# Sixteen transfers inside SBUF in place of a write to DRAM and four reads, for the shifted rows of a depthwise convolution

## The chip, the cores and the metric

One core of a Trainium2 chip runs the kernel. The metric is device time in microseconds, the median of several runs. The profile is of one execution; its times are microseconds from the start of its span. Engines: PE is TensorE, DVE is VectorE, ACT is ScalarE, POOL is GpSimd, SP is the engine from which most transfers are issued (SPq is its queue in the profile).

## The reference

Two layers over 512 tokens of 1024 channels. The change lies in the convolution module of the first layer; what follows it (SwiGLU feed-forward, attention, a second feed-forward) is untouched.

```
def conformer_conv(x, w_pw1, b_pw1, w_dw, b_dw, ln_g, ln_b, w_pw2, b_pw2):
    a = jax.nn.glu(x @ w_pw1 + b_pw1, axis=-1)
    y = lax.conv_general_dilated(                 # depthwise, causal, 31 taps
        a, w_dw[:, None, :].astype(a.dtype), window_strides=(1,),
        padding=((CONV_WIDTH - 1, 0),),
        dimension_numbers=('NWC', 'WIO', 'NWC'),
        feature_group_count=D_MODEL) + b_dw
    y = jax.nn.silu(layernorm(y, ln_g, ln_b))
    return y @ w_pw2 + b_pw2
...
h = h + conformer_conv(rmsnorm(h, norm_mix[l]), ...)
```

For a channel c and a token s the convolution is y[s, c] = sum over j of w[j, c] * apad[c, s + j], where apad is the gated row of the channel with 30 zeros ahead of it.

## The kernel before

Activations lie with channels on the 128 partitions and tokens along the free dimension, so 1024 channels are 8 tiles (numbered 0 to 7, `ct` in the code) of 128x512. Matrix products are made in float32 by three matmuls on a high and a low part of each operand. The weights come in chunks of 128x1024 floats (512 KB), loaded from DRAM into one of four buffers named `raw` (issued from SP, line 285), then split by ACT (`whi`, line 307, a cast) and by DVE (`wlo`, line 307, a subtraction). PE uses the chunks in a fixed order; the first pointwise product uses chunks 2*ct and 2*ct+1 for tile ct, sixteen in all, and the second the next eight. A buffer `raw` can be filled again when its chunk is split.

For each tile, `project` makes the pointwise product in two PSUM banks (PE, line 375, the line of the helper that keeps PE's order), and `gate` makes the gated rows `apad` of 128x542 floats from them (DVE lines 917, 919 and 920, ACT line 918). The 31 taps of a tile are then shared out:

- DVE makes the first taps one by one (`taps`, recorded on line 318, the line of a helper `Turn` that sets an order among operations of one kind).
- ACT and POOL make the next ones (`products`, ACT lines 970 and 973, POOL line 975).
- PE makes the last 12 to 20 in `rounds` (line 956), four taps by one matmul. For this it needs the tile's rows in a second layout, the tile `shifted`: partition s*32+c of column block g holds channel g*32+c, moved by s tokens. A matmul then multiplies 128 rows (32 channels, four shifts) with a 128x32 table. Tile 7 adds four taps by diagonal matrices (`diagonals`) and does its rounds by halves.

`shifted` is made by transfers alone: channels must move to other partitions. In the kernel before, `gate` issues from SP a write of `apad` to a DRAM tile `rowsd`, and then four reads of it, one for each shift s, each into 32 partitions. All of these go through the helper `copies`, a `Turn`, and so stand on line 318. There are four buffers of `shifted` and three of `apad`.

The order of PE's work in this stage is the order of the code: project(0), project(1), project(2) with rounds(0) at its end, then project(3), (4), (5) with rounds(1), (2), (3) each in the second half, then project(6), project(7), rounds(4), (5), (6), the diagonals, sums for the layer norm, and rounds(7). On the other engines and on SP a scheduler sets the order when the program is built. Each engine takes its instructions strictly in that order, and SP takes its transfers so too: one that waits holds up all behind it. The transfers from SP and ACT take their completion semaphores from eight in turn, and a transfer is issued only when the last one with its semaphore has landed, so at most eight are under way.

Of the kernel before, what the change touches and what calls it, by code (L numbers as in the profile page):

```python
# [10 lines left out]
F32 = mybir.dt.float32  # L11
# [6 lines left out]
P = 128  # L18
D = 1024
S = 512  # L20
# [4 lines left out]
PAD = TAPS - 1  # L25
# [159 lines left out]
def hybrid_trunk(ctx: ExitStack, tc: tile.TileContext, xT, W, prm_in, wdw_in, rnd_in, sinks, relb, onehot, fin, out):  # L185
    nc = tc.nc
# [6 lines left out]
    dpool = ctx.enter_context(tc.tile_pool(name="dram", bufs=1, space=DRAM))  # L193
# [3 lines left out]
    def uid(s):  # L197
        ctr[0] += 1
        return f"{s}{ctr[0]}"
# [7 lines left out]
    def temp():  # L207
        return tmp.tile([P, 512], F32, tag="tmp", name=uid("tmp"))
# [234 lines left out]
    def col(name, i):  # L443
        c = PARAM_COLS[name] + i
        return prm[:, c:c + 1]
# [351 lines left out]
    with conv_stage:  # L797
# [58 lines left out]
        for k in range(KT):  # L856
            g = col("mix0", k)
# [26 lines left out]
        copies = Turn()  # L884

        class Conv:
# [24 lines left out]
            def gate(self):  # L911
                ct = self.ct
                rs_bc = rms0.step2()
                a = self.a = cv.tile([P, PAD + S], F32, tag="apad", name=uid("apad"), bufs=3)
                nc.gpsimd.memset(a[:, 0:PAD], 0.0)
                sig = temp()
                nc.vector.tensor_mul(sig, self.gt, rs_bc)
                gated = nc.scalar.activation(sig, sig, AF.Sigmoid, bias=col("b1", KT + ct)).ins
                nc.vector.tensor_mul(self.lin, self.lin, rs_bc)
                self.gated = nc.vector.scalar_tensor_tensor(a[:, PAD:], self.lin, col("b1", ct), sig, op0=ALU.add,  # L920
                                                            op1=ALU.mult).ins
                n = S + 4 * (self.r - 1)
                q = self.q = cv.tile([P, 4, S + 4 * (max(ROUNDS) - 1)], F32, tag="shifted", name=uid("shifted"), bufs=4)
                row = PAD + S
                ad = dpool.tile([P, row], F32, tag=uid("rows"), name=uid("rowsd"))
                copies(nc.sync.dma_start, ad, a)
                for s in range(4):
                    copies(nc.sync.dma_start, q[s * 32:(s + 1) * 32, :, 0:n],
                           bass.AP(tensor=ad.tensor, offset=ad.offset + self.j0 + s,
                                   ap=[[row, 32], [32 * row, 4], [1, n]]))  # L930
                for n in range(self.n_diag):
                    with tc.issue_after(gated):
                        nc.scalar.mul(diag[:, n, :], ident, self.tap(TAPS - self.n_diag + n))
# [555 lines left out]
```

## Time and profile before

| What | Value |
|---|---|
| Median of 3 runs | 1037.89 us (1037.68 to 1038.6) |
| Profiled execution | 1037.62 us, of which 1035.8 us are the span of instructions |
| Granted TensorE clock | 0.999 |
| PE busy | 1023.2 us (99% of the span) |
| DVE, ACT, POOL busy | 815.9, 544.4, 222.1 us |
| Convolution stage on PE | about 11 to 148 us of the span |
| Transfers `rowsd<-apad` | 8, of 271 KB, median 2.6 us from issue to landing |
| Transfers `shifted<-rowsd` | 32, of 260 to 264 KB, medians 4.4 to 5.6 us |

Busy time is the share in which an engine worked; for a kernel whose PE is busy 99% of the time the question for any edit is which PE idle time it removes or adds. Rows of the timeline give start, duration, engine, line, operation, `out<-in`, and in brackets the idle time of the engine before it with what ended it. "To landing" is the time from a transfer's issue to its completion.

### The profile page before, as it was taken

To read this page: it belongs to the slowest core of one execution; us is meant where nothing else is said; L and a number is where in the kernel's file an instruction comes from. 1 tells how busy PE (TensorE), PEld (TensorE's weight loads), DVE (VectorE), ACT (ScalarE), POOL (GpSimd) and SP (SyncE) were. 2 spreads that over 40 slices of the span, in tenths; PEclk is the share of its full clock that TensorE was granted. 3 is DMA by queue.
4 is the path that set the end of the run, shared out by engine and by line. 5 is a ranking of instruction groups with operands and counts; after the bars stand their busy time and mean duration, and the time that the engine had idled before them with its cause. 6 is when DMAs were issued, how large, how long until landed. Compare 5 with 4: busy or idle time off the path is not lost.

```text
span 1035.8 us, 17669 instructions
## 1 busy us (share of the span) xinstructions
PE 1023.2 (99%) x7016; PEld 912.4 (88%) x7016; DVE 815.9 (79%) x1144; ACT 544.4 (53%) x847; POOL 222.1 (21%) x249
## 2 busy tenths in 40 slices
PE   8999999999999999999999999999999999999997
PEld 7766568888999999999998778788989999999996
DVE  7889867589789888988997677578956888789863
ACT  7566745434554555455565666344534654555443
POOL 0799811311001010010000534141200001010000
PEclk9999999999999999999999999999999999999999
DMA  7766542366557975785473120641664459666612
GB/s 242 204 158 159 131 129 82 108 177 163 153 137 190 269 185 142 234 209 138 102 235 92 61 62 21 178 110 38 162 223 129 117 137 261 187 147 171 178 41 82
DMA packets 51055, 153.95 MB, mean 149 GB/s; under 512 B 5979, under 2 KB 8844, under 8 KB 50956
## 3 DMA queue, kind: packets, MB, share of 16 engines
q1 hardware_dynamic: 41756, 124.79, 38.1%
q0 software_dynamic: 8064, 26.74, 15.0%
q10 hardware_dynamic: 1152, 1.29, 0.4%
q8 instruction: 55, 0.90, 0.3%
q14 instruction: 28, 0.23, 0.1%
HBM read 148.46 MB, written 6.83 MB: 150 GB/s over the span
## 4 chain that ended last, share of the span: by engine, by line
PE 93%; DMA 3%; DVE 2%; ACT 1%; issue 0%; SPq 0%; DVEq 0%; ACTq 0%
PE bank L383 23%; PE bank L384 23%; PE bank L385 23%; PE bank L375 21%; PE bank L1418 2%; DMA rowsd<-apad 1%; DVE wlo L307 1%; DMA h<-in_xT_dram 1%; DMA shifted<-rowsd 1%; ACT tmp L318 0%; DMA raw<-in_W_dram 0%; PE bank L1408 0%; ACT quad L318 0%; DMA prm<-in_prm_dram 0%; ACT whi L307 0%
## 5 line engine op out<-in xcount | busy, mean ns | idle before, releaser
L384 PE MATMUL bank<-quad,whi 128*128 128x256 f32 (+1 forms) x1572 | 472.4, 302 | 0.0
L385 PE MATMUL bank<-quad,wlo 128*128 128x256 f32 (+1 forms) x1572 | 469.6, 302 | 0.0
L383 PE MATMUL bank<-quad,whi 128*128 128x256 f32 (+1 forms) x1572 | 465.7, 302 | 0.0
L384 PEld LDWEIGHTS bank<-quad,whi 128*128 128x128 f32 x1572 | 300.0, 191 | 11.1
L383 PEld LDWEIGHTS bank<-quad,whi 128*128 128x128 f32 x1572 | 298.4, 191 | 11.2
L385 PEld LDWEIGHTS bank<-quad,wlo 128*128 128x128 f32 x1572 | 298.2, 191 | 11.0
L307 ACT CAST whi<-raw 128x1024 fp32r<-128x1024 f32 (+1 forms) x184 | 184.0, 1002 | 214.2 <-PE bank L384 123.3
L307 DVE TENSOR_TENSOR wlo<-raw,whi 128x1024 fp32r<-128x1024 f32 (+1 forms) x184 | 224.9, 1227 | 82.5 <-ACT whi L307 79.8
L375 PE MATMUL bank<-quad,whi 128*128 128x512 f32 x512 | 161.0, 395 | 2.4 <-ACT whi L318 0.9
L241 POOL DMA_DIRECT2D blocks<-in_W_dram x56 | 49.5, 907 | 460.6 <-DMA blocks<-in_W_dram 169.3
L307 ACT CAST whi<-blocks 128x1024 fp32r<-128x1024 f32 (+1 forms) x84 | 81.6, 972 | 111.3 <-PE bank L384 81.8
L375 PEld LDWEIGHTS bank<-quad,whi 128*128 128x128 f32 x512 | 94.4, 188 | 29.1 <-issue 5.1
L307 DVE TENSOR_TENSOR wlo<-blocks,whi 128x1024 fp32r<-128x1024 f32 (+1 forms) x84 | 94.1, 1124 | 10.1 <-ACT whi L307 9.3
L375 PE MATMUL bank<-quad,wlo 128*128 128x512 f32 x256 | 99.9, 390 | 0.1
L975 POOL TENSOR_TENSOR quad<-quad 128x512 f32<-128x512 f32 x53 | 76.6, 1445 | 13.3 <-ACT quad L973 10.2
L375 PEld LDWEIGHTS bank<-quad,wlo 128*128 128x128 f32 x256 | 48.0, 188 | 10.9 <-DVE wlo L318 0.7
L611 DVE TENSOR_TENSOR h<-h,bank 128x512 f32<-128x512 f32 x70 | 46.8, 680 | 10.7 <-PE bank L385 10.6
L973 ACT ACTIVATE quad<-apad,wdw 128x512 f32<-128x512 f32 x53 | 36.9, 718 | 20.0 <-POOL quad L975 20.0
L1317 POOL TENSOR_SCALAR sc<-sc,sm 128x256 f32<-128x256 f32 (+1 forms) x64 | 31.8, 519 | 58.9 <-DVE sm L1315 58.8
L517 DVE TENSOR_TENSOR quad<-tmp,quad 128x512 fp32r<-128x512 f32 (+1 forms) x62 | 41.0, 662 | 2.3 <-ACT quad L516 2.1
L516 ACT CAST quad<-tmp 128x512 fp32r<-128x512 f32 (+1 forms) x62 | 35.1, 584 | 13.7 <-POOL tmp L655 7.6
L1313 ACT ACTIVATE sc<-sc,m 128x257 f32<-128x257 f32 (+1 forms) x64 | 30.3, 475 | 22.2 <-DVE m L1304 22.2
(192 smaller groups left out, 1216.2 us busy)
## 6 DMA issues: line engine op xcount, KB each, us to landing
raw<-in_W_dram SPq DMA_DIRECT2D x109, 512.0 KB, 3.8
blocks<-in_W_dram SPq DMA_DIRECT2D x54, 512.0 KB, 6.0
blocks<-in_W_dram POOLq DMA_DIRECT2D x36, 512.0 KB, 7.6
blocks<-in_W_dram SPq DMA_DIRECT2D x30, 384.0 KB, 3.9
raw<-in_W_dram SPq DMA_DIRECT2D x21, 384.0 KB, 3.7
blocks<-in_W_dram POOLq DMA_DIRECT2D x20, 384.0 KB, 5.9
shifted<-rowsd SPq DMA_DIRECT2D x16, 262.0 KB, 4.4
shifted<-rowsd SPq DMA_DIRECT2D x12, 260.0 KB, 5.3
```

Source lines behind the costliest of these rows:

```text
L241: nc.gpsimd.dma_start(f[:, j, 0:w], part(1 - j, 1 - j), accum_op=ALU.add)
L307: done = (nc.scalar.copy(hi, r).ins, lo_engine[0].tensor_sub(lo, r, f32(hi)).ins)
L375: turn[0] = nc.tensor.matmul(*args, **kw).ins
L383: nc.tensor.matmul(out, w[0], x[0], start=start, stop=False, **kw)
L384: nc.tensor.matmul(out, w[0], x[1], start=False, stop=False, **kw)
L385: nc.tensor.matmul(out, w[1], x[0], start=False, stop=stop, **kw)
L516: nc.scalar.copy(dst[0], src)
L517: nc.vector.tensor_sub(dst[1], src, f32(dst[0]))
L611: nc.vector.tensor_tensor(t, t, src.rearrange("p (m s) -> p m s", m=2), op=op)
L973: nc.scalar.mul(pr, src, self.tap(j))
L975: nc.gpsimd.tensor_add(to, acc, pr)
L1317: nc.gpsimd.tensor_scalar(sc[:, j, 1:1 + w], sc[:, j, 1:1 + w], sm[:, j:j + 1], 0.0, op0=ALU.mult, op1=ALU.add)
```

## The change

The write to DRAM and the four reads are taken out. In their place stand sixteen transfers from `apad` to `shifted`, one for each shift s and each block g of 32 channels, 32 rows of 2080 to 2112 bytes each. The three lines on `rowsd` go.

```
                 q = self.q = cv.tile([P, 4, S + 4 * (max(ROUNDS) - 1)], F32, tag="shifted", name=uid("shifted"), bufs=4)
-                row = PAD + S
-                ad = dpool.tile([P, row], F32, tag=uid("rows"), name=uid("rowsd"))
-                copies(nc.sync.dma_start, ad, a)
                 for s in range(4):
-                    copies(nc.sync.dma_start, q[s * 32:(s + 1) * 32, :, 0:n],
-                           bass.AP(tensor=ad.tensor, offset=ad.offset + self.j0 + s,
-                                   ap=[[row, 32], [32 * row, 4], [1, n]]))
+                    for g in range(4):
+                        copies(nc.sync.dma_start, q[s * 32:(s + 1) * 32, g, 0:n],
+                               a[g * 32:(g + 1) * 32, self.j0 + s:self.j0 + s + n])
```

The scheduler puts some instructions in another order. PE's order is the same in both programs. On SP, from the copies of tile 0 to those of tile 2, these rows stand before (raw_439, 469, 559 and 589 are chunks 9 to 12, raw_682 and raw_712 chunks 13 and 14; apad_334, 400 and 513 are tiles 0, 1 and 2):

```order
L318 DMA rowsd_342<-apad_334 128x542
L285 DMA raw_439<-in_W_dram 128x1024
L318 DMA shifted_341<-rowsd_342 32x4x520 x4
L285 DMA raw_469<-in_W_dram 128x1024
L285 DMA raw_559<-in_W_dram 128x1024
L285 DMA raw_589<-in_W_dram 128x1024
L318 DMA rowsd_408<-apad_400 128x542
L318 DMA shifted_407<-rowsd_408 32x4x524 x4
L285 DMA raw_682<-in_W_dram 128x1024
L318 DMA rowsd_521<-apad_513 128x542
L285 DMA raw_712<-in_W_dram 128x1024
L318 DMA shifted_520<-rowsd_521 32x4x520 x4
```

After the change the same stretch of SP reads so (raw_459, 489, 589, 619 are chunks 9 to 12, raw_722 and raw_752 chunks 13 and 14; apad_334, 410 and 533 are tiles 0, 1 and 2):

```order
L318 DMA shifted_341<-apad_334 32x520 x16
L318 DMA shifted_417<-apad_410 32x524 x16
L285 DMA raw_459<-in_W_dram 128x1024
L285 DMA raw_489<-in_W_dram 128x1024
L285 DMA raw_589<-in_W_dram 128x1024
L285 DMA raw_619<-in_W_dram 128x1024
L285 DMA raw_722<-in_W_dram 128x1024
L285 DMA raw_752<-in_W_dram 128x1024
L318 DMA shifted_540<-apad_533 32x520 x16
```

Chunks 9 to 12, which went out ahead of tile 1's copies, now stand behind all 32 transfers of tiles 0 and 1, and chunk 14 moved ahead of tile 2's copies.

On DVE, around the gating of tile 2 (line 920 with apad_513), these rows stand before; wlo_592 and wlo_685 are the low parts of chunks 9 and 10, and line 992 adds the rounds of tile 0:

```order
L307 TENSOR_TENSOR wlo_592<-raw_439,whi_591 128x1024
L917 TENSOR_TENSOR tmp_515<-bank_438,rsbc_182 128x512
L919 TENSOR_TENSOR bank_437<-bank_437,rsbc_182 128x512
L920 SCALAR_TENSOR_TENSOR apad_513<-bank_437,prm,tmp_515 128x512
L307 TENSOR_TENSOR wlo_685<-raw_469,whi_684 128x1024
```

After the change (line 992 is line 989 there) they read:

```order
L917 TENSOR_TENSOR tmp_535<-bank_458,rsbc_182 128x512
L307 TENSOR_TENSOR wlo_622<-raw_459,whi_621 128x1024
L919 TENSOR_TENSOR bank_457<-bank_457,rsbc_182 128x512
L307 TENSOR_TENSOR wlo_725<-raw_489,whi_724 128x1024
L920 SCALAR_TENSOR_TENSOR apad_533<-bank_457,prm,tmp_535 128x512
```

The split of chunk 10 now stands ahead of tile 2's gating instead of behind it, and line 917 ahead of the split of chunk 9.

## The prediction

> **What bounds the kernel now.** I read the page first, then who PE waited for in the convolution stage, then the busy time by stretch.
>
> ```profile
> PE 1023.2 (99%) x7016; PEld 912.4 (88%) x7016; DVE 815.9 (79%) x1144; ACT 544.4 (53%) x847; POOL 222.1 (21%) x249
> ```
>
> PE is the bound: all its idle time in the span is 1035.8 - 1023.2 = 12.6 us. Only idle time that hangs on these copies can be won. In the stretch from 20 to 150 us PE's waits are:
>
> ```profile
> PE bank L375 <- DMA shifted<-rowsd: 1.2, 2, 0.9
> PE bank L534 <- ACT quad L318: 0.8, 1, 0.8
> PE bank L375 <- DVE mv L318: 0.3, 1, 0.3
> ```
>
> The columns are total, count and longest. The copies cost PE 1.2 us in two waits. Busy time by stretch (window, its length, PE busy, and so on) shows nothing else hidden:
>
> ```profile
> 43.00:62.00 19.00, 18.05 (x105) 10.90 (x106) 14.94 (x20) 11.22 (x16) 17.20 (x15) 1.00 0.63 177
> 62.00:130.00 68.00, 68.00 (x366) 42.85 (x365) 60.84 (x74) 44.63 (x66) 63.30 (x48) 1.00 0.62 153
> 20.00:150.00 130.00, 127.83 (x736) 84.94 (x735) 108.10 (x134) 76.46 (x111) 94.48 (x71) 1.00 0.62 161
> ```
>
> From 62 to 130 us PE has no gap at all. The whole stage has 130 - 127.83 = 2.17 us of idle time. PE's starts of the rounds are the deadlines of the copies:
>
> ```profile
> 43.71 2.78 PE L375 MATMUL bank<-shifted,tables 128*32 128x512 f32 x24 [0.91 <-DMA shifted<-rowsd]
> 55.16 3.64 PE L375 MATMUL bank<-shifted,tables 128*32 128x512 f32 x32 [0.24 <-DMA shifted<-rowsd]
> 70.83 2.78 PE L375 MATMUL bank<-shifted,tables 128*32 128x512 f32 x24
> 86.43 3.64 PE L375 MATMUL bank<-shifted,tables 128*32 128x512 f32 x32
> 118.76 9.65 PE L375 MATMUL bank<-shifted,tables 128*32 128x512 f32 x88
> 134.62 0.66 PE L375 MATMUL bank<-shifted,tables 128*32 128x256 f32 x8
> ```
>
> The rows are tiles 0, 1, 2, 3, then 4 to 6 together, then 7. Only tiles 0 and 1 came late, by 0.91 and 0.24 us, 1.15 us together. That is the most that copies which are early enough can give; the rest of the span follows PE, so it is carried to the end.
>
> **What the old copies cost.** SP's queue (x is the number of issues in the row; its duration is theirs):
>
> ```profile
> 31.85 0.33 SPq L318 DMA_DIRECT2D rowsd<-apad  x1
> 34.16 1.76 SPq L318 DMA_DIRECT2D shifted<-rowsd  x4
> 36.04 3.00 SPq L285 DMA_DIRECT2D raw<-in_W_dram  x3
> 40.06 0.33 SPq L318 DMA_DIRECT2D rowsd<-apad  x1
> 47.80 1.76 SPq L318 DMA_DIRECT2D shifted<-rowsd  x4
> 59.23 0.34 SPq L318 DMA_DIRECT2D rowsd<-apad  x1
> 61.81 1.74 SPq L318 DMA_DIRECT2D shifted<-rowsd  x4
> 73.63 0.35 SPq L285 DMA_DIRECT2D raw<-in_W_dram  x1
> 74.33 0.34 SPq L318 DMA_DIRECT2D rowsd<-apad  x1
> 114.49 0.34 SPq L318 DMA_DIRECT2D rowsd<-apad  x1
> 124.31 0.34 SPq L318 DMA_DIRECT2D rowsd<-apad  x1
> 126.67 1.73 SPq L318 DMA_DIRECT2D shifted<-rowsd  x4
> 131.41 27.08 SPq L285 DMA_DIRECT2D raw<-in_W_dram  x6
> ```
>
> A write goes out as soon as the rows are gated. Undisturbed, the reads follow 2.3 to 2.6 us later; tile 1's write at 40.06 stood behind the three weight loads of the row at 36.04, and its reads waited until 47.80. The rate of tile 1's reads, from the DMA view of 47.8 to 55.2 us in 40 slices of 0.185 us:
>
> ```profile
> GB/s 0 0 0 0 0 125 34 159 181 385 374 363 227 238 181 227 181 181 181 193 193 272 238 227 227 238 181 227 181 193 159 125 68 45 0 0 0 0 0 0
> DMA packets 576, 1.07 MB, mean 145 GB/s; under 512 B 64, under 2 KB 64, under 8 KB 576
> ```
>
> Data begins about 0.9 us after the first issue, moves mostly at some 200 GB/s, ends near 54.0, and PE starts at 55.16: 7.2 us from first issue to use. So the old way needs 2.4 + 7.2 = 9.6 us after gating, undisturbed.
>
> **The new copies.** Each is a quarter of a read, 66.6 KB: 0.33 us of data at 200 GB/s. No transfer inside SBUF is in this trace, so issue and landing are bounded by the nearest rows:
>
> ```profile
> L318 SPq DMA_DIRECT2D shifted<-rowsd x32: 302/424/433, 34.2 to 128.0; - x32
> DMA to landing us min/median/max: 3.4/5.2/7.2
> rowsd<-apad SPq DMA_DIRECT2D x8, 271.0 KB, 2.6
> raw<-in_W_dram SPq DMA_DIRECT2D x16, 512.0 KB, 4.5
> raw<-in_W_dram SPq DMA_DIRECT2D x2, 512.0 KB, 6.0
> ```
>
> The first row is issue time in ns, the second the landing of the same reads; the two last are weight loads, all of 20 to 135 us and those of 39 to 58 us, in a fuller queue. Issue spacing: 0.35 us (0.302 plus a gap of 0.05) to 0.46 us (1.76 us for four, and a little for the semaphore); I take 0.40, nearer the simple rows of 0.33 to 0.34. Landing: from 2.3 us (the lowest of the writes, as the gap 31.85 to 34.16 shows) to 3.4 us (the lowest of the 262 KB reads). I take 2.4, which is 3.4 less the 0.98 us that the other three quarters take at 200 GB/s. With eight semaphores in turn the ninth issue waits for the first landing: 8 x 0.40 = 3.2 us is above 2.4, so no wait. Sixteen copies then land 15 x 0.40 + 2.4 = 8.4 us after gating, bounds 7.6 and 10.3.
>
> The Trainium skill speaks against this: "DMA: Bandwidth & Descriptors", Rules for kernel authors, says to coalesce small transfers, since near 64 KB one pays mostly overhead, and its section on the anatomy of one DMA puts 2.0 us fixed on each, an estimate of 2.15 us for 66.6 KB. By that landing the sixteen would take 8.15 us instead of 8.4; that the fixed part overlaps is borne out here by four reads in 7.2 us.
>
> Tile by tile, with PE 1.15 us earlier from tile 1 on:
> - Tile 0: 31.85 + 8.4 = 40.3 (upper 42.2), needed at 43.71 - 0.91 = 42.8. Its stall goes, also at the upper bound.
> - Tile 1: SP is free at 38.3, so 40.06 + 8.4 = 48.5, needed at 54.0. Its stall goes.
> - Chunks 9 to 12, which stand behind these 32 copies: issued from 40.06 + 16 x 0.40 = 46.5, so chunk 9 lands at 46.5 + 4.5 = 51.0. ACT casts it when its products are done, as before (below, at 53.87). Hidden, by 2.9 us.
> - Tile 2 is the tightest. Rows of ACT and DVE there:
>
> ```profile
> 53.87 1.03 ACT L307 CAST whi<-raw 128x1024 fp32r<-128x1024 f32 x1
> 54.93 2.08 DVE L307 TENSOR_TENSOR wlo<-raw,whi 128x1024 fp32r<-128x1024 f32 x1 [3.33 <-ACT whi L307]
> 56.94 0.68 DVE L917 TENSOR_TENSOR tmp<-bank,rsbc 128x512 f32<-128x512 f32 x1
> 57.54 0.68 DVE L919 TENSOR_TENSOR bank<-bank,rsbc 128x512 f32<-128x512 f32 x1
> 58.41 0.76 DVE L920 SCALAR_TENSOR_TENSOR apad<-bank,prm,tmp 128x512 f32<-128x512 f32 x1 [0.18 <-ACT tmp L918]
> 57.65 0.72 ACT L918 ACTIVATE tmp<-tmp,prm 128x512 f32<-128x512 f32 x1 [2.75 <-DVE tmp L917]
> 59.35 1.27 DVE L307 TENSOR_TENSOR wlo<-raw,whi 128x1024 fp32r<-128x1024 f32 x1 [0.19 <-ACT whi L307]
> ```
>
> Line 917 moves into DVE's wait of 3.33 us, and ACT's line 918 (0.7 us) ahead of its cast, so the cast ends at 55.65; then 2.08 + 0.6 + 1.2 + 0.75 gives rows gated at 60.3, where before they were at 59.17: 1.1 later. Just ahead, when chunk 10 is split at 59.5, SP issues chunk 14, which lands at 64.0. The eighth copy has the semaphore of that load, and so waits for its landing; eight more issues and a landing give 64.0 + 3.2 + 2.4 = 69.6, needed at 70.83 - 1.15 = 69.7. Just in time: I cost it at nothing, bounds -0 and +1.4 us (a load that takes 6.0 us instead of 4.5).
> - Tile 3: chunk 16 goes out at 73.63, lands at 78.1, the rest of the copies at 78.1 + 5.6 = 83.7, needed at 85.3.
> - Tile 6: 114.49 + 8.4 = 122.9 (upper 124.8). Its rounds begin 28/44 into the row at 118.76, at 124.9 - 1.15 = 123.75.
> - Tile 7: 132.7 (upper 134.6), needed at 133.5. SP's last issue at 124.31 + 6.4 = 130.7 is ahead of the load at 131.41, so the loads of the next product are not moved.
>
> At the upper bounds tiles 6 and 7 would take the 1.15 us back but not more. The eight writes and 2.2 MB of DRAM traffic that fall away free nothing that PE waits for. The sum: 1037.62 (the profiled execution) - 0.91 - 0.24 + 0.05 for tile 2 = 1036.5; that execution lies 0.27 us under the median, so 1036.8.
>
> **The rivals.**
> - *Gained at the start, lost at tile 2 (or 6, 7)*: chunk 14 ahead of the copies, landing after 6 us, makes tile 2 ready at 71.1, 0.3 later than the old start: 1038.1. For it: a margin of 0.1 us. Against it: DMA queues that are emptier than before at that time.
> - *Slower: a copy takes 0.66 us, not 0.40*, because both its ends lie on 32 partitions and the data rate is halved to 100 GB/s. Before, only the destination lay on 32 partitions, and 200 GB/s stand against the 360 to 385 of the slices at the start. Tile 0's issues end at 42.4, tile 1's at 53.0, chunk 9 lands at 57.5 instead of 51.0, is cast and split by 60.6, tile 2 is gated at 63.2, and its copies land at 63.2 + 10.6 + 2.4 = 76.2: 5.4 us after 70.83, so 1043.3. It decides from about 0.6 us a copy; under that, tile 2 is less than 2 us late. Against it: reads and writes need not share a path, and the issue rows are far below.
>   The Trainium skill, "SBUF — State Buffer", section on the DMA port swizzle, has 32 partitions reach 8 of 16 ports, 189 GB/s for 1 MiB; the 200 GB/s here agree. It does not say what a copy with both ends so placed does, and no row here shows it.
> - *Slower by far: the copies run one after another*, 2.3 us each: 16 x 2.3 = 37 us a tile, 294 us for eight from 31.85 on, 326 in place of 134: about 1230. The four reads in flight together speak against it.
>   The coalescing rule of the Trainium skill ("DMA: Bandwidth & Descriptors", Rules for kernel authors) would lead there if the fixed parts did not overlap.
> - *Faster*: the moved splits would have to remove all 2.17 us of idle time in the stage: 1035.7. The waits at lines 534 and 375 (DVE mv) come from the layer norm behind the rounds, so hardly.
>
> **How the numbers follow.** About 0.2% (2.1 us) is what a measurement of this kernel can tell from no change. Likeliest (both stalls gone, 1036.8): 0.64. Lost at tiles 2, 6 or 7 (1037 to 1038.3): 0.20. Spacing of 0.6 us or more: 0.12. One after another: 0.01. Faster than 0.2%: 0.03. So faster 0.03, same 0.84, slower 0.13. The range starts at 1036.2 (all 1.15 us, and a low run) and reaches past the second case to 1039.5, into the third; beyond it lies somewhat over 0.1.
>
> **What would show it.** PE's wait on `shifted` is gone at the rounds of tiles 0 and 1; rows of 16 issues on SP take about 6.4 us; copies land in about 2.4 us; tile 2's rounds start at 69.7 with no wait; line 920 of tile 2 ends near 60.3; the casts of chunks 9 and 10 wait for no load. Wrong is the prediction if issues are 0.6 us apart or more (then tile 2's rounds wait for a copy and DVE for chunk 9), or if landing times grow so that SP waits on its own transfers.

## The result and the profile after

| | Before | After |
|---|---|---|
| Median | 1037.79 us (1037.62 to 1038.6) | 1046.97 us (1044.41 to 1048.82, four runs) |
| Profiled execution, its span | 1037.62, 1035.8 us | 1044.41, 1042.4 us |
| PE busy | 1023.2 us | 1027.2 us |
| SP's sixteen issues of a tile (five before) | 2.1 us | 10.1 us and more |

The changed kernel is slower: the ratio is 1.0088, with a 95% interval of 1.0076 to 1.0100. The forecast was 1036.8 us and a range up to 1039.5; it was wrong. The profiled execution is the lowest of the four, so the two traces differ by 6.6 us of span where the medians differ by 9.2.

The copies themselves, from the view of the tile `shifted` in the kernel after (issue time in ns as min/median/max, then the time to landing):

```profile
L318 SPq DMA_DIRECT2D shifted<-apad x128: 507/589/1206, 31.5 to 138.1; - x128
DMA to landing us min/median/max: 1.9/2.0/6.0
```

An issue takes 0.589 us, where a read from DRAM took 0.424. Landing is better than forecast: 2.0 us in the median. SP's queue shows what the first number does; the rows answer to those of SP in the prediction:

```profile
31.52 20.62 SPq L318 DMA_DIRECT2D shifted<-apad  x32
52.23 9.28 SPq L285 DMA_DIRECT2D raw<-in_W_dram  x6
61.88 11.39 SPq L318 DMA_DIRECT2D shifted<-apad  x16
107.16 31.55 SPq L318 DMA_DIRECT2D shifted<-apad  x48
138.82 6.31 SPq L285 DMA_DIRECT2D raw<-in_W_dram  x5
```

Thirty-two issues hold SP from 31.52 to 52.14, 0.64 us each with the gaps between. Chunk 9's load goes out at 52.23; before it was at 32.98. Near the end 48 issues in a row hold SP until 138.7, and the first load of the second product (chunk 20) goes out at 138.82 instead of 131.41.

Now what the late loads do on ACT and DVE around the gating of tile 2, and then PE's rounds of tiles 0, 1, 2 and of 4 to 6 and the start of the second product (line 534), which in the last row is that of the kernel before:

```profile
56.27 1.04 ACT L307 CAST whi<-raw 128x1024 fp32r<-128x1024 f32 x1 [2.00 <-DMA raw<-in_W_dram]
61.08 0.74 DVE L920 SCALAR_TENSOR_TENSOR apad<-bank,prm,tmp 128x512 f32<-128x512 f32 x1
```

```profile
42.31 3.59 PE L375 MATMUL bank<-shifted,tables 128*32 128x512 f32 x24
54.21 3.64 PE L375 MATMUL bank<-shifted,tables 128*32 128x512 f32 x32
72.87 5.20 PE L375 MATMUL bank<-shifted,tables 128*32 128x512 f32 x24 [2.45 <-DMA shifted<-apad]
122.15 11.45 PE L375 MATMUL bank<-shifted,tables 128*32 128x512 f32 x88
155.31 0.50 PE L534 MATMUL bank<-quad,whi 128*128 128x512 f32 x1 [0.77 <-ACT quad L318]
```

```profile
148.40 0.50 PE L534 MATMUL bank<-quad,whi 128*128 128x512 f32 x1 [0.77 <-ACT quad L318]
```

ACT waits 2.00 us for chunk 9, tile 2 is gated at 61.82 instead of 59.17, its sixteen copies take 11.39 us, and PE waits 2.45 us for them. The rounds that follow take 5.20 us instead of 2.78: a wait between two matmuls of one row is inside the row's duration. The stalls of tiles 0 and 1 are indeed gone, though tile 0's rounds, 3.59 us instead of 2.78, give 0.8 of the 0.91 us back.

How late PE is against before, by the ends of these rows: tile 1 is 0.95 us early (57.85 against 58.80), tile 2 is 4.46 us late (78.07 against 73.61), the rounds of tiles 4 to 6 are 5.19 us late (133.60 against 128.41), and the second product (line 534) starts 6.91 late (155.31 against 148.40). So there are two places: about 5.4 us at tile 2, and 3.6 us at tiles 6 and 7 and just behind them. Half of the 3.6 is in the row of tiles 4 to 6, 11.45 us instead of 9.65: tile 6's last copies come one by one. Between the two places about 1.1 us comes back, at a spot that is explained with the last experiment. Of the 0.95 us by which tile 1 is early, 0.42 is not the copies' doing: PE is that much ahead of the kernel before already at 26 us (eight small matmuls of line 375 start at 26.33 against 26.75), ahead of any copy.

The chain of waits of the kernel after has the same two places (start, duration, what):

```profile
52.23 3.95 DMA raw<-in_W_dram
61.19 6.35 DMA raw<-in_W_dram
70.78 1.99 DMA shifted<-apad
72.87 65.46 PE bank L375 x344
138.33 0.49 ACT quad L1014
138.82 3.63 DMA raw<-in_W_dram
142.47 1.05 ACT whi L307
```

First chunk 9's load, then chunk 14's, which held the semaphore of the eighth copy for 6.35 us (SP waited 1.0 us of them), then the copy with which PE could begin; at the end chunk 20's load and its cast. The chain puts a square on ACT (line 1014) ahead of that load, but where the load is issued from ACT, in an experiment below, it goes out ahead of the same square; here it follows SP's last issue, which ended at 138.71. Its buffer was free at 136.0, when DVE ended a split begun at 134.32. So of the 7.4 us by which chunk 20 is late, about 4.6 follow PE's own lateness and 2.8 are SP's queue. Behind that cast, in ACT's order, stands the copy of a bank (line 1026) that PE waits for:

```profile
PE bank L375 <- DMA shifted<-apad: 2.5, 1, 2.5
PE bank L375 <- ACT tmp L1026: 0.9, 1, 0.9
```

Last, by stretch (length, busy PE, weight load, DVE, ACT, POOL, granted clock, DMA share, GB/s), the clock behind the wait:

```profile
72.00:76.00 4.00, 3.13 (x13) 1.43 (x17) 2.25 (x2) 2.65 (x4) 3.75 (x5) 0.57 0.58 139
```

If the lower clock is a half, 0.57 over 4 us is about 3.4 us of it; the stretches of 4 us on both sides have 1.00. In the mean over the span the two highest of the four runs have a clock of 0.994, the two lowest 0.996 and 0.997; 0.002 to 0.003 of 1045 us is 2 to 3 us, a large part of the 2.7 to 4.4 us between them. Where such periods fell in the runs without a trace is not seen; some traces below have one at the tail, which this one has not.

### The profile page after: what moved, and what is told of

Same layout as the page of the kernel before. It is cut to its first block, busy times and chain, and to the rows that moved or that the text cites. A ratio compares the mean times of both kernels' runs of the same rounds, so it can differ in the third digit from the quotient of the medians.

```text
span 1042.4 us, 17805 instructions
## 1 busy us (share of the span) xinstructions
PE 1027.2 (99%) x7016; PEld 915.3 (88%) x7016; DVE 813.1 (78%) x1144; ACT 544.6 (52%) x847; POOL 220.3 (21%) x249
## 3 DMA queue, kind: packets, MB, share of 16 engines
q10 hardware_dynamic: 1152, 1.29, 0.4%
## 4 chain that ended last, share of the span: by engine, by line
PE 91%; DMA 3%; DVE 3%; ACT 2%; issue 1%; SPq 0%; POOL 0%; POOLq 0%; DVEq 0%; ACTq 0%
PE bank L384 23%; PE bank L383 23%; PE bank L385 23%; PE bank L375 19%; DMA raw<-in_W_dram 2%; PE bank L1415 2%; DVE wlo L307 1%; DVE bank L318 1%; DMA h<-in_xT_dram 1%; ACT whi L307 0%; ACT tmp L318 0%; DMA prm<-in_prm_dram 0%; ACT quad L318 0%; SPq L318 0%; PE bank L1405 0%
## 5 line engine op out<-in xcount | busy, mean ns | idle before, releaser
L307 DVE TENSOR_TENSOR wlo<-raw,whi 128x1024 fp32r<-128x1024 f32 (+1 forms) x184 | 221.0, 1206 | 90.8 <-ACT whi L307 87.8
```

The costliest lines, as they stand in the source:

```text
L307: done = (nc.scalar.copy(hi, r).ins, lo_engine[0].tensor_sub(lo, r, f32(hi)).ins)
```

## The experiments

In all comparisons below the kernel before ran beside on the same chip (medians of 1037.1 to 1037.5 us). The kernel after did not, and its four runs spread over 4.4 us; so what a version gains on it is read from the two ratios to the kernel before, 0.001 being 1.04 us.

**The cut alone.** The write to DRAM stays, and each of its four reads is cut into four.

```
-                    copies(nc.sync.dma_start, q[s * 32:(s + 1) * 32, :, 0:n], bass.AP(... ap=[[row, 32], [32 * row, 4], [1, n]]))
+                    for g in range(4):
+                        copies(nc.sync.dma_start, q[s * 32:(s + 1) * 32, g, 0:n], bass.AP(... ap=[[row, 32], [1, n]]))
```

> The kernel before, with each of the four reads of a tile cut into four (32 rows of 520 to 528 floats), so sixteen reads from DRAM behind the write. Theory 'source': an issue is dear (0.59 us) because both ends lie in SBUF. Then these issues take 0.31 to 0.43 us, sixteen take 5.5 to 7 us, a tile is ready some 8.7 us after its first read: tile 1 at 47.8 + 8.7 = 56.5 (1.3 later than before), tile 7 at 126.7 + 8.7 = 135.4 (0.8 later): 1038 to 1040.5 us. Rival 'shape': any transfer of one block of 32 rows costs 0.59 us to issue, spacing 0.645: sixteen take 10.3 us, tile 2 is ready at 61.8 + 9.7 + 2.4 = 73.9 (3.1 late), tile 7 at 138.8: 1043 to 1048 us.

1041.51 us, ratio 1.0040 (1.0025 to 1.0055). An issue takes 0.419 us and sixteen take 7.29 us, 0.46 apart, the forecast's upper bound (view of `shifted`, then SP's timeline):

```profile
L318 SPq DMA_DIRECT2D shifted<-rowsd x128: 302/419/2042, 33.3 to 133.5; - x128
```

```profile
33.28 7.29 SPq L318 DMA_DIRECT2D shifted<-rowsd  x16
134.09 6.51 SPq L285 DMA_DIRECT2D raw<-in_W_dram  x5
```

So the issue of the same 32 rows is dearer by 0.17 us where they come from SBUF. The time was above what was expected. Chunk 20 is late here too, at 134.09: PE waits 1.04 us for the copy of the bank, and over 142 to 146 us its clock is 0.57. Tile 6's reads are late as well, and its 32 matmuls take 5.04 us instead of 3.64. These places had not been counted.

**A first probe of kinds of transfers.** Five extra transfers, one of each kind, behind the reads of tiles 4 and 5 of the kernel before.

```
+                if ct in (4, 5):
+                    copies(nc.sync.dma_start, y[7][0:32, :], a[32:64, 0:512])      # SBUF to SBUF
+                    copies(nc.sync.dma_start, y[7][32:64, :], ad[32:64, 0:512])    # DRAM to SBUF
+                    copies(nc.sync.dma_start, y[6], a[:, 0:512])                   # SBUF to SBUF, 128 rows
+                    copies(nc.sync.dma_start, sd, a[32:64, 0:512])                 # SBUF to DRAM
+                    copies(nc.sync.dma_start, y[7][64:96, 0:64], a[32:64, 0:64])   # SBUF to SBUF, 8 KB
```

> The kernel before, with five more transfers behind the reads of tiles 4 and 5, where SP is idle; they write rows that are overwritten later. Issue times, theory 'source': 32x512 within SBUF 0.5 to 0.6 us, 32x512 from DRAM to SBUF 0.31 to 0.43, 128x512 within SBUF 0.5 to 0.6 or more, 32x512 from SBUF to DRAM 0.31 to 0.34, 32x64 within SBUF 0.5 to 0.6. Rival 'shape': the three of 32x512 alike. Rival 'crowd' (an issue is dear only among sixteen in a row): all 0.31 to 0.43. Time as before, within 1 us.

Two of the rows of SP's timeline:

```profile
91.23 0.62 SPq L318 DMA_DIRECT2D quad<-apad  x1
91.91 0.56 SPq L318 DMA_DIRECT2D quad<-rowsd  x1
```

Inconclusive: all five took 0.52 to 0.62 us, even the read from DRAM in the second row, which takes 0.42 among its like. So what an issue costs seems to hang on the one ahead of it too. The kernel after bears this out: a single weight load right behind a row of copies takes 0.52 us there (at 73.38), and 0.33 to 0.34 where no copy is just ahead (at 61.19 and 76.21). Kinds must not be mixed.

**Tile 7 by the old way.** The kernel after, but tile 7 by a write and four reads (`if ct in (0, 1, 2, 3, 4, 5, 6):` around the sixteen copies).

> The changed kernel with tile 7 alone made by the old write and reads. Theory 'tail': of the 6.9 us by which the second product starts later in the changed kernel (155.31 against 148.40), 4.5 stood at the end of tile 2's rounds (78.00 against 73.54), and 2.4 came at the end, where the load of chunk 20 stands behind tile 7's copies and ACT waits for it. Then this kernel is 2 to 2.5 us faster than the changed one, about 1044.5 us median, and chunk 20 goes out within 3 us of tile 7's last read. Rival: the tail only follows tile 2's delay, and the time stays at 1046 to 1048 us.

1043.28 us, ratio 1.0057 (1.0040 to 1.0073): by the ratios 3.2 us less than the kernel after, by intervals that only just part. Chunk 20 goes out at 136.94, and the wait for the copy of the bank is gone. So the tail is a place of its own. The wait at tile 2 stays as it was (PE's waits, then SP's timeline):

```profile
PE bank L375 <- DMA shifted<-apad: 2.7, 1, 2.7
```

```profile
136.94 6.34 SPq L285 DMA_DIRECT2D raw<-in_W_dram  x5
```

**PE kept busy.** Ten extra 128x128 matmuls, whose results are not used, ahead of tile 2's rounds, to see whether the half clock makes those rounds long.

```
+                if self.ct == 2:
+                    for _ in range(10):
+                        in_turn(c[:, 0:P], ones_m, ones_m, start=True, stop=True, skip_group_check=True)
```

> The changed kernel with ten 128x128 matmuls of constants (some 2.4 us) ahead of tile 2's rounds, into the bank that the rounds overwrite; they fill PE's wait of 2.45 us. Theory 'clock': PE's idle time there made the granted clock drop to a half for 3.4 us, and the 24 instructions of the rounds took 5.20 us instead of 2.78. Then they take about 2.8 to 3 us here, the granted clock stays at 1.00 from 72 to 76 us, and the time falls by 1.5 to 2.4 us, to about 1045 us, with less spread. Rival 'arrival': the rounds are slow since copies 14 to 16 land 0.6 us apart: they still take about 5 us and the time stays.

1047.6 us, ratio 1.0095: no gain. The clock is whole at tile 2, and its rounds end at 77.65 instead of 78.07 (the stretch with its clock, then PE's timeline):

```profile
72.00:76.00 4.00, 4.00 (x29) 1.98 (x31) 2.24 (x2) 2.65 (x4) 3.65 (x5) 1.00 0.58 139
```

```profile
73.06 4.59 PE L375 MATMUL bank<-shifted,tables 128*32 128x512 f32 x24
```

Of the 2.4 us by which these rounds were longer, 1.8 stay with a whole clock: copies 14 to 16 arrive one by one, 0.63 us apart. The half clock there costs 0.4 to 0.6 us. The time does not fall by even that; in this trace a period of low clock stands elsewhere: at the tail PE waits 1.10 us for the copy of the bank, and then the second half of tile 7's rounds takes 3.51 us, where the kernel after has 2.37 (the stretch, then PE's timeline):

```profile
146.00:150.00 4.00, 4.00 (x45) 2.09 (x45) 0.00 (x0) 0.00 (x0) 0.00 (x0) 0.67 0.38 133
```

```profile
146.33 3.51 PE L375 MATMUL bank<-shifted,tables 128*32 128x256 f32 x40
```

**Chunk 20 from another queue.** The kernel after, with that one load issued from ACT: `(nc.scalar if i == 20 else nc.sync).dma_start(...)`.

> The changed kernel with one load moved: chunk 20 goes out from ACT instead of SP, so that it does not stand behind tile 7's copies. The copies stay as they are. Theory 'tail': it goes out when its buffer is free, about 3 us sooner than at 138.8, ACT's cast of it no longer holds up the copy of the sums that PE waits for, and the time falls by 2 to 4 us against 1047, as it did with tile 7 by the old way. Rival 'copies': tile 7's rounds themselves come too late, and nothing is won.

1045.41 us, ratio 1.0076 (1.0059 to 1.0093). That interval overlaps the one of the kernel after (1.0076 to 1.0100): a gain is not shown, and the expected 2 to 4 us did not come. The load goes out at 136.6 from ACT, 2.2 us earlier, but its 512 KB are then under way together with tile 7's last copies. The copy that PE needs takes 4.99 us to land, where in the kernel after those of this place took 2.0 to 2.1, and PE, which did not wait for tile 7's copies there, now does (from the chain of waits, then PE's timeline):

```profile
136.89 4.99 DMA shifted<-apad
```

```profile
142.01 3.42 PE L375 MATMUL bank<-shifted,tables 128*32 128x256 f32 x40 [1.30 <-DMA shifted<-apad]
```

So at the tail the load and the copies are in each other's way: in one queue by the order of issue, in two by the time to landing.

**Tiles 0 to 2 by the old way**, tiles 3 to 7 by the new.

> The changed kernel with tiles 0, 1 and 2 by the old write and reads, tiles 3 to 7 by sixteen transfers. Theory of two places (tile 2, and the tail behind tile 7): the loss at tile 2 is gone, the tail's is not: chunk 20 goes out at about 134.5 instead of 131.4, and the time is 1040 to 1042 us. Rival 'one place' (all follows from tile 2): within 0.5 us of before.

1041.81 us, ratio 1.0046 (1.0031 to 1.0062). By the ratios that is 4.4 us under the kernel after; the loss at tile 2 less what comes back behind it is 5.4 - 1.1 = 4.3. At the end the wait for the copy of the bank stands again, 1.3 us, and behind it the clock is 0.61 over 142 to 146 us.

**Only tiles 3 to 6 by the new way.**

> Only tiles 3 to 6 by sixteen transfers, 0 to 2 and 7 by the old way. Theory of two places: neither is touched. By the spacing of 0.634 us tile 3's last copy lands at 74.3 + 9.5 + 2.4 = 86.2, as it is needed at 86.4, and tile 6's at 114.5 + 9.5 + 2.4 = 126.4, 1.5 us after 124.9: so 1037.5 to 1039.5 us. Rival 'everywhere' (the transfers cost wherever they stand, by DMA or by SP's time): over 1040 us.

1039.46 us, ratio 1.0021 (1.0011 to 1.0031). Both big places are gone; what stays is that tiles 5 and 6 follow one another in SP's queue (32 issues, 22.54 us), so that tile 6's copies come late to its rounds (timelines of PE and SP):

```profile
125.18 1.69 PE L375 MATMUL bank<-shifted,tables 128*32 128x512 f32 x4 [0.39 <-DMA shifted<-apad]
102.99 22.54 SPq L318 DMA_DIRECT2D shifted<-apad  x32
```

**The order on SP put right.** The kernel after, with chunks 9 and 10 ahead of tile 1's copies and chunk 20 from ACT.

```
+                if half == 1 and n == 3 and ct == 2:
+                    with tc.issue_after(last_load[0]):
+                        convs[1].shift()
```

> The changed kernel with chunk 20 from ACT and with tile 1's copies behind the loads of chunks 9 and 10 instead of ahead of them; all tiles by sixteen transfers. Theory: chunk 9 goes out at about 42 instead of 52, ACT does not wait for it, tile 2 is gated at about 59.5 instead of 61.8, its copies land at about 71.7 instead of 75: of the 4.5 us lost at tile 2 some 2.5 come back, and with the tail the time is 1040.5 to 1042.5 us. Rival 'spacing alone' (tile 2 is late by its own sixteen issues, not by when it was gated): no better than chunk 20 from ACT alone.

1042.11 us, ratio 1.0046 (1.0031 to 1.0061): the expected time, but by another sum. Tile 2 loses nothing, where 2 us were expected to stay: it is gated at 58.60, and its rounds begin without a wait and last as long as before. What chunk 14's load does is not told apart here, since in this program it stands behind tile 2's copies as well. The tail lost more than expected: tile 6's 32 matmuls wait 0.46 us and take 5.42 instead of 3.64, and tile 7's copies, with chunk 20's load under way, are late again:

```profile
70.55 2.78 PE L375 MATMUL bank<-shifted,tables 128*32 128x512 f32 x24
137.84 3.18 PE L375 MATMUL bank<-shifted,tables 128*32 128x256 f32 x40 [1.01 <-DMA shifted<-apad]
```

**Two queues.** The kernel after, with half of each tile's copies issued from ACT: `copies((nc.sync, nc.scalar)[g % 2].dma_start, ...)`.

> The sixteen copies of each tile in two queues, eight issued from SP and eight from ACT; nothing else in the text of the changed kernel differs (the scheduler sets ACT's and DVE's rows anew around them). Theory that the issue pace of the one queue sets it all: each queue still needs about 0.63 us a copy, both at once, so a tile goes out in about 5 us instead of 10; chunk 9's load goes out near 42 us instead of 52, tile 2's rounds start without a wait, and the copies of tiles 5 to 7 hold SP half as long, so chunk 20 goes out near 131 us. Time 1036.5 to 1039, where the upper end is what ACT's 5 us a tile of issuing may cost the products that it makes for POOL. Rival, the copies hinder one another in the DMA engines or in SBUF and not at issue: two queues at once get about 1.2 us a copy each, nothing moves, 1044 to 1049.

1047.89 us, ratio 1.0102 (1.0088 to 1.0116): the time was missed by 9 us, and the rival failed as well. Each queue kept the pace of one alone, and landing stayed at 2.1 us, although together they moved mostly about 200 GB/s (162 in the mean over 32 to 43 us) against 99 in the kernel after. So up to that rate the copies do not hinder one another; the issue is the limit, each queue for itself. The view of `shifted` here, then the DMA view of 32 to 43 us here, and the DMA view of 31.5 to 52.2 us in the kernel after:

```profile
L318 SPq DMA_DIRECT2D shifted<-apad x64: 507/592/834, 32.2 to 136.1; - x64
L318 ACTq DMA_DIRECT2D shifted<-apad x64: 514/602/846, 32.3 to 135.8; - x64
```

```profile
DMA packets 1267, 1.78 MB, mean 162 GB/s; under 512 B 417, under 2 KB 417, under 8 KB 1266
```

```profile
DMA packets 1449, 2.05 MB, mean 99 GB/s; under 512 B 480, under 2 KB 480, under 8 KB 1447
q1 hardware_dynamic: 1447, 2.02, 41.8%
```

Chunk 9's load goes out at 43.25, near the 42 expected, and no round waits for a copy. But a row of eight issues holds up ACT as it holds up SP, tile after tile: before seven products ACT waits 27.7 us in all. ACT's timeline, and then PE's waits:

```profile
32.26 5.08 ACTq L318 DMA_DIRECT2D shifted<-apad  x8
37.39 0.82 ACT L967 ACTIVATE quad<-apad,prm,wdw 128x512 f32<-128x512 f32 x1 [5.12 <-DMA shifted<-apad]
47.69 1.03 ACT L307 CAST whi<-raw 128x1024 fp32r<-128x1024 f32 x1
```

```profile
PE bank L375 <- DVE apad L920: 2.3, 1, 2.3
```

The products wait 5.12 us, the cast that stood at 34.10 in the kernel after comes at 47.69, and tile 2 is gated at 63.14, later than there (61.82). The cost moved to an engine on which PE waits by another way.

**A second probe**, each kind in a row of its own: `copies(nc.sync.dma_start, y[i], a[:, 0:512])` three times behind tile 4's reads; four of `sd[...]` from `a[...]` and four of 32x64 within SBUF behind tile 5's.

> The kernel before with extra transfers on SP whose data nobody uses: behind tile 4's reads three of 128 rows of 2 KB from SBUF to SBUF; behind tile 5's reads four of 32 rows of 2 KB from SBUF to DRAM and then four of 32 rows of 256 bytes from SBUF to SBUF. Each kind stands in a row of its own, so that only the first of a kind follows another kind. Theory that both ends in SBUF make the issue dear, whatever the shape: the two kinds within SBUF take 0.55 to 0.60 us each from the second on, the four to DRAM 0.40 to 0.47. Rival, a transfer of 32 rows is dear: the 128-row ones take 0.33 to 0.35 and both kinds of 32 rows 0.55 to 0.60. Second rival, any source in SBUF is dear: the four to DRAM take 0.55 to 0.60 too.

The views of the tiles written, for the three kinds in the order of the text (ns as min/median/max):

```profile
L318 SPq DMA_DIRECT2D quad<-apad x3: 575/576/617, 89.9 to 91.2; - x3
L318 SPq DMA_DIRECT2D scrd<-apad x4: 414/431/456, 106.8 to 108.2; - x4
L318 SPq DMA_DIRECT2D quad<-apad x4: 507/524/591, 108.7 to 112.1; - x4
```

Both ends in SBUF make an issue dear, 0.51 to 0.62 us, a little under what was expected for the small ones; rows and bytes hardly do (262 KB or 8 KB), and one end in DRAM takes 0.41 to 0.46 in a row. Three in a row are as dear as sixteen, so it is not the crowd either.

**The gain without the copies.** The kernel before, with the loads of chunks 9 and 10 behind tile 1's reads: `with tc.issue_after(copies.last) if 9 <= i <= 10 else nullcontext():` around the load.

> The kernel before with the loads of chunks 9 and 10 put behind tile 1's four reads on SP, where they stood ahead of them. What the predicted gain was: PE's waits of 0.91 us for tile 0's reads and 0.24 us for tile 1's. Theory that these waits come from the three loads of 512 KB that share the DMA engines with the reads, and that chunks 9 and 10 are not needed until 53 us: both waits go and nothing is late, 1.0 to 1.2 us less than before, 1036.0 to 1036.5 in the scale of these runs. Rival, the two chunks become late for their split and tile 2 is gated later: within 0.5 us of before or slower.

1037.52 us, ratio 1.0001 (0.9992 to 1.0010): nothing. The two stalls are gone, and a new one stands at tile 2 (PE's timeline):

```profile
70.70 2.78 PE L375 MATMUL bank<-shifted,tables 128*32 128x512 f32 x24 [1.10 <-DMA shifted<-rowsd]
```

**That stall taken away too**, with chunk 14 behind tile 3's reads (`i in (9, 10, 14)`).

> As the last one (the kernel before, chunks 9 and 10 behind tile 1's reads), and chunk 14 moved too, from between tile 2's write and its reads to behind tile 3's reads, with chunks 15 and 16, which follow it in SP's order. In the last kernel the two old waits were gone, but a new one of 1.1 us stood at tile 2's rounds. Theory that tile 2's reads land late because the 512 KB of chunk 14 are ahead of them in the DMA engines, and that this bounds what any earlier start is worth: that wait goes, tile 2's rounds start near 69.6 instead of 70.7, and the time falls by up to 1.1 us, 1036.1 to 1036.6 where before is 1037.2. Rival, something other than chunk 14 sets tile 2's reads, or a later place gives the microsecond back as well: 1036.9 to 1037.6, with the wait at tile 2 or another one in its place.

1037.48 us, ratio 1.0001 (0.9992 to 1.0010): the rival. Tile 2's rounds now start at 69.46 without a wait, and PE waits for POOL 36 us later. Here are the sums for the layer norm between the products, from PE's timeline in the kernel before (its second row is from the weight loads that go with them, PEld), in the kernel after, and in this one (here the last four of eight):

```profile
105.05 2.68 PE L375 MATMUL bank<-quad,ones_m 128*32 128x512 f32 x8
106.02 0.14 PEld L375 LDWEIGHTS bank<-quad,ones_m 128*32 128x32 f32 x2 [0.83 <-POOL quad L994]
```

```profile
109.49 1.58 PE L375 MATMUL bank<-quad,ones_m 128*32 128x512 f32 x8
```

```profile
106.01 1.71 PE L375 MATMUL bank<-quad,ones_m 128*32 128x512 f32 x4 [1.19 <-POOL quad L994]
```

In the kernel after, where they start 4.4 us later, the eight take 1.58 us. Before, the row has 2.68: at least 1.1 us of waiting that is counted as PE's work. The weight load names what for already in the kernel before, and the last row names the same: POOL's `quad`. Both before and here the sums end at 107.7. So a microsecond won ahead of this spot could not be kept, and of the 4.4 us lost ahead of it 1.1 comes back.

## Why the prediction was wrong

- *Issue spacing, the step that failed.* It took 0.40 us, bounds 0.35 to 0.46, from loads and reads that have one end in DRAM. It is 0.59 for the issue and 0.63 with the gap, past the 0.6 that the prediction named as its sign of being wrong; the second probe shows that both ends in SBUF make it so. The upper bound stood on rows of another kind, and the probability of 0.12 for 0.6 us and more was too small for an operation that no row showed.
- *Landing* (2.4, bounds 2.3 to 3.4): 2.0 in the median, up to 6.0 at tile 2, where chunk 14's load was under way. "Sixteen copies 8.4 us after gating" became 15 x 0.63 + 2.0, about 11.5. Tiles 0 and 1 made it nevertheless, tile 0 with its last copies late by 0.8.
- *Chunk 9 "hidden, by 2.9 us"*: its load went out 5.7 us later than the 46.5 forecast, and ACT waited 2.0. This, not the copies of tile 2 alone, began the loss: with chunks 9 and 10 put ahead (and chunk 14 behind), tile 2's rounds do not wait, though its copies are issued at the same pace.
- *Tile 2 "at nothing", bounds -0 and +1.4*: 5.4 us from the end of tile 1's rounds to the end of tile 2's, of which 2.45 are the wait for the copies, 2.4 the longer rounds and 0.4 a wait for the gating. The semaphore behind chunk 14's load was foreseen; it took 6.35 us, more than the 4.5 of the sum and the 6.0 of its bound, and cost SP 1.0 us.
- *"The loads of the next product are not moved"*: wrong for the same reason. 6.4 us a tile became 10.5, the three last tiles in a row held SP until 138.7, and chunk 20 was 7.4 us late, 2.8 of them by that queue. With tile 7 by the old way, some 3 us of the loss are gone.
- *The rival of 0.66 us a copy* had the pace and the way to tile 2 nearly right, and the wrong cause. It had tile 2's copies land at 76.2, where the last landed at about 74.7; that its 5.4 us is also the loss measured over tile 2's rounds is chance, since the two count different stretches. The data rate was no limit: SP's packets took 41.8% of the DMA engines' time in the kernel after (the row `q1` above), and two queues moved some 200 GB/s, twice the rate on which this rival rests. Its time of 1043.3 lacks the tail, and what the lower clock adds in some runs.
- *The gain of 0.91 and 0.24 us* would not have come even with copies fast enough. Two places stood behind it: tile 2's reads, and POOL at 107 us. "PE has no gap from 62 to 130 us" was read from busy time, in which the wait for POOL does not show; the rows of the weight loads show it.
- The rule of the Trainium skill on coalescing ("DMA: Bandwidth & Descriptors", Rules for kernel authors) had the right sign, though the copies lie just above its 64 KB. The fixed time of about 2.0 us a transfer in the section of that page on the anatomy of one DMA (for transfers from GpSimd) agrees with the landing of 2.0 us, but that overlapped; the price here was the issue. The cut alone cost 4.1 us (1041.51 against 1037.45).

Still open: why an issue with both ends in SBUF takes 0.17 us longer. No run shows what SP does in that time. No run shows either what decides whether a wait of PE is followed by half clock. No version was faster than the kernel before by more than the noise.

## What to carry to other kernels

Count the issues of a queue as work of that queue: number times pace, with the pace from a row of the same kind (both ends), and then look at what stands behind them in order; here the copies' issues made weight loads late, and these in turn made the next copies late. A price that no row shows needs a measurement or a wide bound, above all when a table of due times is met by tenths of a microsecond. And before a stall is counted as a gain, find the next place where PE would wait: compare the duration of equal rows (2.68 against 1.58 us for eight matmuls) and look at the weight loads among them, since a wait inside a row looks like work. An order that takes a load out of the copies' way in the queue can still put it in their way in the time to landing (4.99 us against 2.0).

## What the runs showed of the hardware

- A transfer from SBUF to SBUF takes SP or ACT 0.52 to 0.60 us to issue (medians of the rows above), from 8 KB to 262 KB nearly alike; one with an end in DRAM 0.41 to 0.46 in a row of several, 0.30 to 0.35 alone, but 0.51 to 0.59 right behind one from SBUF to SBUF. Two queues issue at once without slowing one another (0.592 and 0.602 us), but ACT started nothing else during a row of eight (5.12 us). Single issues between its products did not slow these: from 38.11 us on they came every 0.62 us, as without issues.
- A copy of about 65 KB that went out 0.3 us behind a load of 512 KB from the other queue took 4.99 us to land; without such a load it is 2.0.
- A wait of PE of 2.45 us, followed by matmuls with gaps, was enough for some 3.4 us at half clock. The Trainium skill ("TensorE: Matmul & The Clock Gate", Part 1) puts this down to a free-running window of about that length in which PE was idle; the length agrees, and the window need not have been idle throughout. Ten small matmuls in the gap kept the clock at 1.00. The length of a wait does not decide it alone: behind waits of 1.04 to 1.29 us among small matmuls at the tail the clock fell (0.57, 0.61 and 0.67 over 4 us in three runs), behind 0.90 us in the kernel after and 1.30 us with chunk 20 from ACT it stayed at 1.00.
